# An order table of a hybrid Conformer and Mamba-2 layer: the last z tile before the LayerNorm, the last x tile after it in the list

## The chip, the core and the metric

One Trainium2 chip, one of its cores. The metric is the device time of one launch in microseconds, the median of several runs. The matrix engine is called PE (TensorE), the others DVE (VectorE), ACT (ScalarE), POOL (GpSimd); SP (SyncE) issues most DMAs.

## What is computed

One layer over a prompt of 1,040 rows (16 meta tokens and 1,024) and 32 sample rows (8 sequences of 4), model width 1,024, all in float32, followed by a gated ConvFFN and a final norm:

```python
u = _rmsnorm(h, g_mix)
proj = u @ w_in                                   # 1024 -> 4624 columns
glu = conf_in[..., :1024] * sigmoid(conf_in[..., 1024:])
c, conf_buf = _causal_dwconv(conf_prev, glu, conf_w, conf_b)      # width 31
c = silu(_layernorm(c, ln_g, ln_b))
xbc_c, xbc_buf = _causal_dwconv(xbc_prev, xbc, sconv_w, sconv_b)  # width 4
xbc_c = silu(xbc_c)                               # x (16 heads), B and C (2 groups)
y, h_ssm = _ssd(xs, dt, A, Bm, Cm, d_skip, ssm_prev)              # chunks of 128 rows
y = _group_rmsnorm(y * silu(z), snorm_g)
h = h + concat([c, y]) @ w_out
up, ffn_buf = _causal_dwconv(ffn_prev, _rmsnorm(h, g_ffn) @ w_up, fconv_w, fconv_b)
h = h + (silu(up[..., :2816]) * up[..., 2816:]) @ w_down
```

## The kernel before, in words

**Layout.** Activations lie transposed, channels on the 128 partitions and the 1,072 rows along the free axis. Every product is made of three matmuls on a split into a high and a low part (`products`, lines 215 to 217), in three column chunks of 358, 358 and 356 rows; a weight tile of 128 output columns has 8 blocks of 128 rows, so 3 x 8 x 3 = 72 matmuls make one projection tile. A weight tile is loaded (L189, `wr`), its high part made on ACT (L204, `wh`), its low part on DVE (L205, `wl`); each of these has two buffers.

**Items.** Up to the output projection the program is a list of items, `ORDER` (line 59), that a loop emits one after the other. `p0` to `p7` (`emit_pair`) are the Conformer's channel tiles: two projections, the GLU, and the convolution of width 31, made of two halves (even rows `fp`, L532 and L535; odd rows `fo`, L533 and L538) and of a third sum `fs` of both (L539, L541), put together by L544 to L547 into `gq`. `x0` to `x11` (`emit_xbc`) are the tiles of x, B and C: projection, evacuation to `fb` (L558, L560), four taps into `xo` (L575 on ACT, three L577 on DVE), silu (L579, L580), and two stores to `x_d` in memory (L581, L582). `z0` to `z7` (`emit_z`) are the gate's tiles: projection, evacuation (L589), silu (L592), store to `z_d`. `s0` and `s1` are one chunk of head group 0 or 1 of the SSD scan, which loads its x, B and C back from `x_d` (L673, L674), makes transposes (L679, L696), L697 to L700 and products; `q` is the sample rows' chunk, `r` their states. The head groups: x0 to x3, x8 and x10 are group 0's; x4 to x7, x9 and x11 are group 1's, of which x9 is its B; z4 to z7 are group 1's too. Each `l` is one block of 256 columns (the fifth has 48) of the LayerNorm over channels (`ln_part`): transposes of `gq` (L862), statistics (L863, L866), 1/sqrt (L156 on DVE, L157 on POOL, L868), normalized values `cn` (L874 on DVE, L876 on ACT), transposes back (L883), silu (L884). `h` splits the result, `c0` to `c7` are the tiles of the output projection over it.

**What sets the order.** Within an engine, instructions run in the order of its queue. A scheduler sets that order from a priority for each instruction: by default the place in the list, with some put ahead (`prio(URGENT)`: evacuations, weight splits), the taps of an x tile by a fixed 500 (`XP`), and the Conformer's taps by a fixed 1,000,000 (`CVP`), behind other work. So `ORDER` alone doesn't tell where an item comes to stand on each engine. Buffers limit it too: `fb` has two, shared with the sample chunk's `kept` and the sample state's `rr`; `xo` has two, shared with z tiles; `fp`, `fo`, `fs` and `fz` have one each.

Of the kernel before, what the change touches and what calls it, by code (L numbers as in the profile page):

```python
# [55 lines left out]
LNP = None  # L56
XP = 500
PMM, PBK, PSM = 2, 4, 2
ORDER = ("p0 p1 z1 z0 x10 p2 x8 x0 x2 p3 p4 x6 z2 p5 x3 dt x7 x1 z3 s0 s0 s0 p6 s0 s0 s0 p7 x5 x4 x11 x9 s0 q0 s0 z4 z7 z6 l l z5 l l l h s1 s1 c0 s1 r0 s1 s1 q1 s0 c2 s1 c3 s1 s1 c4 s1 s0 c5 s1 c6 y0 y1 r1 c7")


@with_exitstack
def hybrid_kernel(ctx: ExitStack, tc: tile.TileContext, a: dict, outs: list):
# [907 lines left out]
    lns, hs = ExitStack(), ExitStack()  # L971
    items = ORDER.split()
    last_ssd = max(i for i, t in enumerate(items) if t[0] in "sq")
# [571 lines left out]
```

## Time and profile before

| | |
|---|---|
| median of 3 runs | 1611.01 us (1605.16, 1611.01, 1611.17) |
| profiled execution | 1602.27 us, span 1600.6 us, mean granted PE clock 0.98 |
| PE, its weight loads | busy 96%, 92% |
| DVE, ACT, POOL | busy 73%, 56%, 3% |
| DMA | 209.90 MB, 131 GB/s over the span |

Busy shares are over the whole span, so a stage where PE waits is seen only in the windows. In the timeline, a row's first two numbers are its start and its duration in microseconds from the span's start; a bracket at the end is the idle time of the engine just before it, and what ended it.

### The profile page before, as it was taken

How to read it: one execution, taken by the hardware profiler on the slowest of the kernel's cores; microseconds unless marked ns; L12 is line 12 of the kernel's file. 1: busy time of each engine (PE TensorE's matmuls, PEld its weight loads, DVE VectorE, ACT ScalarE, POOL GpSimd, SP SyncE). 2: the span in 40 equal slices, each digit the busy share in tenths (PEclk: the TensorE clock that was granted, in tenths of full speed). 3: DMA queues.
4: the chain of work that ended last, by engine and by line, in shares of the span. 5: the costliest groups of instructions: out<-in, count | busy, mean ns of one | idle time of the engine just before them, and what ended most of it. 6: DMA issues, size and time to landing. Idle time of an engine off the chain costs nothing.

```text
span 1600.6 us, 28038 instructions
## 1 busy us (share of the span) xinstructions
PE 1536.9 (96%) x10716; PEld 1479.4 (92%) x10716; DVE 1164.3 (73%) x1881; ACT 895.7 (56%) x2160; POOL 40.4 (3%) x99
## 2 busy tenths in 40 slices
PE   6899999999999799998999999999999999999997
PEld 5899999997999688887999999999999998999997
DVE  4799989996897758465668787777777776464343
ACT  6635545478968576684335556656655665353232
POOL 2000000000000000000000000000000000000000
PEclk9999999999999899999989999999999999999998
DMA  6321312166435329667753222222222228766553
GB/s 245 112 69 58 99 45 72 57 179 160 111 115 155 101 70 268 184 172 237 241 171 107 90 84 90 81 73 70 76 83 80 83 79 273 231 204 198 154 161 108
DMA packets 306229, 209.90 MB, mean 131 GB/s; under 512 B 28453, under 2 KB 285017, under 8 KB 306079
## 3 DMA queue, kind: packets, MB, share of 16 engines
q1 hardware_dynamic: 302654, 198.26, 41.8%
q0 software_dynamic: 1056, 5.24, 0.9%
q10 hardware_dynamic: 2384, 4.60, 0.8%
q8 instruction: 84, 1.38, 0.4%
q14 instruction: 51, 0.41, 0.1%
HBM read 157.69 MB, written 51.22 MB: 131 GB/s over the span
## 4 chain that ended last, share of the span: by engine, by line
PE 81%; DMA 6%; issue 5%; DVE 4%; ACT 2%; POOL 1%; SPq 1%; POOLq 0%; DVEq 0%; ACTq 0%
PE mm L216 11%; PE mm L215 11%; PE mm L217 11%; PE X L1249 5%; PE X L1250 5%; PE X L1251 5%; PE mmd L1429 3%; PE mmd L1427 3%; PE mmd L1428 3%; PE Z L1251 2%; PE Z L1250 2%; PE Z L1249 2%; PE Y L1250 1%; PE Y L1249 1%; PE Y L1251 1%
## 5 line engine op out<-in xcount | busy, mean ns | idle before, releaser
L204 ACT CAST wh<-wr 128x768 fp32r<-128x768 f32 (+1 forms) x130 | 131.1, 1009 | 253.6 <-PE mm L216 107.1
L215 PE MATMUL mm<-u_hi,wh 128*128 128x358 f32 (+1 forms) x816 | 268.8, 329 | 0.9 <-ACT sg L245 0.9
L217 PE MATMUL mm<-u_hi,wl 128*128 128x358 f32 (+1 forms) x816 | 268.3, 329 | 0.0
L216 PE MATMUL mm<-u_lo,wh 128*128 128x358 f32 (+1 forms) x816 | 267.6, 328 | 0.0
L205 DVE TENSOR_TENSOR wl<-wr,wh 128x768 fp32r<-128x768 f32 (+1 forms) x130 | 152.4, 1173 | 109.5 <-ACT wh L204 105.2
L1250 PE MATMUL X<-tq,wh 128*128 128x264 f32 (+1 forms) x640 | 183.4, 287 | 0.0
L1249 PE MATMUL X<-tq,wh 128*128 128x264 f32 (+1 forms) x640 | 183.0, 286 | 0.0
L1251 PE MATMUL X<-tq,wl 128*128 128x264 f32 (+1 forms) x640 | 182.7, 285 | 0.0
L1429 PE MATMUL mmd<-g,wl 128*128 128x352 f32 x528 | 171.4, 325 | 1.8 <-DVE wl L205 1.8
L1427 PE MATMUL mmd<-g,wh 128*128 128x352 f32 x528 | 171.5, 325 | 0.9 <-ACT wh L204 0.9
L1428 PE MATMUL mmd<-g,wh 128*128 128x352 f32 x528 | 169.8, 322 | 0.0
L215 PEld LDWEIGHTS mm<-u_hi,wh 128*128 128x128 f32 x816 | 153.6, 188 | 1.6 <-ACT sg L245 1.1
L217 PEld LDWEIGHTS mm<-u_hi,wl 128*128 128x128 f32 x816 | 154.0, 189 | 0.6 <-issue 0.3
L216 PEld LDWEIGHTS mm<-u_lo,wh 128*128 128x128 f32 x816 | 153.5, 188 | 0.5 <-issue 0.4
L1250 PEld LDWEIGHTS X<-tq,wh 128*128 128x128 f32 x640 | 121.7, 190 | 0.0
L1249 PEld LDWEIGHTS X<-tq,wh 128*128 128x128 f32 x640 | 120.9, 189 | 0.3 <-ACT arena L1267 0.3
L1251 PEld LDWEIGHTS X<-tq,wl 128*128 128x128 f32 x640 | 121.0, 189 | 0.0
L1342 DVE SCALAR_TENSOR_TENSOR cv<-arena,ffnv,cv 128x528 f32<-128x528 f32 (+1 forms) x88 | 67.8, 771 | 65.7 <-ACT cv L1339 65.7
L1429 PEld LDWEIGHTS mmd<-g,wl 128*128 128x128 f32 x528 | 99.3, 188 | 3.4 <-DVE wl L205 3.3
L1267 ACT COPY arena<-X 128x266 f32<-128x266 f32 (+2 forms) x200 | 63.2, 337 | 69.4 <-PE X L1251 66.7
L1427 PEld LDWEIGHTS mmd<-g,wh 128*128 128x128 f32 x528 | 99.2, 188 | 1.5 <-ACT wh L204 1.1
L1428 PEld LDWEIGHTS mmd<-g,wh 128*128 128x128 f32 x528 | 99.7, 189 | 0.0
(337 smaller groups left out, 3885.8 us busy)
## 6 DMA issues: line engine op xcount, KB each, us to landing
wr<-in_w_down_dram SPq DMA_DIRECT2D x48, 512.0 KB
wr<-in_w_in_dram SPq DMA_DIRECT2D x36, 512.0 KB
wr<-in_w_out_dram SPq DMA_DIRECT2D x24, 512.0 KB
wr<-in_w_up_dram SPq DMA_DIRECT2D x24, 512.0 KB
spare<-in_w_up_dram SPq DMA_DIRECT2D x20, 512.0 KB
wr<-in_w_down_dram SPq DMA_DIRECT2D x24, 384.0 KB
ab<-acs_d SPq DMA_DIRECT2D x32, 256.0 KB
h<-in_state_ssm_dram SPq DMA_DIRECT2D x32, 256.0 KB
```

Source lines behind the costliest of these rows:

```text
L204: nc.scalar.copy(hi[:, :kk, :], raw[:, :kk, :])
L205: nc.vector.tensor_tensor(lo[:, :kk, :], raw[:, :kk, :], hi[:, :kk, :].bitcast(F), op=ALU.subtract)
L215: mm = [nc.tensor.matmul(ps[:, :n], hi[:, k, :], xh, start=(j == 0), stop=False), nc.tensor.matmul(ps[:, :n], hi[:, k, :], xl, start=False ...
L216: nc.tensor.matmul(ps[:, :n], hi[:, k, :], xl, start=False, stop=False),
L217: nc.tensor.matmul(ps[:, :n], lo[:, k, :], xh, start=False, stop=(j == kk - 1))]
L1249: tick([nc.tensor.matmul(ps[:, :n], hi[:, k, :], bh[:, k, :], start=start and k == 0, stop=False, **kw), nc.tensor.matmul(ps[:, :n], hi[:, ...
L1250: nc.tensor.matmul(ps[:, :n], hi[:, k, :], bl[:, k, :], start=False, stop=False, **kw),
L1251: nc.tensor.matmul(ps[:, :n], lo[:, k, :], bh[:, k, :], start=False, stop=(k == 3), **kw)])
L1342: nc.vector.scalar_tensor_tensor(co[:, j0:nj], fb[:, k + j0:k + nj], ffnv[:, m, 16 + k:17 + k], co[:, j0:nj], op0=ALU.mult, op1=ALU.add)
L1427: nc.tensor.matmul(ps[:, :n], hi[:, k, :], xh, start=(k0 + k == 0), stop=False)
L1428: nc.tensor.matmul(ps[:, :n], hi[:, k, :], xl, start=False, stop=False)
L1429: nc.tensor.matmul(ps[:, :n], lo[:, k, :], xh, start=False, stop=(k0 + k == KF - 1))
```

## The change

In the list, `x9` goes from behind `x11` to between the second and the third LayerNorm block, and `z5` from there to ahead of the first one. Nothing else differs.

```diff
-... s0 p7 x5 x4 x11 x9 s0 q0 s0 z4 z7 z6 l l z5 l l l h s1 s1 c0 s1 r0 ...
+... s0 p7 x5 x4 x11 s0 q0 s0 z4 z7 z6 z5 l l x9 l l l h s1 s1 c0 s1 r0 ...
```

**PE, from x11 to the first LayerNorm block.** The number behind `wh` names the weight tile: before, `wh_4782` is x9 and `wh_5666` is z5. `xc_4886` is group 0's chunk 6, `xc_5958` group 1's first chunk. Before:

```order
L217 MATMUL mm_4739<-u_hi1_126,wl_4684 128x356
L215 MATMUL mm_4786<-u_hi0_125,wh_4782 128x358
...
L679 MATMUL ptx_4889<-ident_88,xc_4886 128x128 x4
...
L215 MATMUL mm_5670<-u_hi0_125,wh_5666 128x358
...
L217 MATMUL mm_5722<-u_hi1_126,wl_5667 128x356
L696 MATMUL pbt_5978<-ident_88,xc_5958 128x128
L697 MATMUL pbt_5978<-xc_5958 128x128
L883 MATMUL pb_5565<-ident_88,cn_5541 128x128
```

With the change (`wh_5646` is x9, `wh_5151` is z4, and the one chunk 6 reads is `xc_4777`):

```order
L215 MATMUL mm_5155<-u_hi0_125,wh_5151 128x358
...
L215 MATMUL mm_5650<-u_hi0_125,wh_5646 128x358
...
L217 MATMUL mm_5702<-u_hi1_126,wl_5647 128x356
L472 MATMUL pe_5731<-ident_88,ex_4666 81x128
L862 MATMUL pt_5508<-ident_88,gq1_130 128x128
L862 MATMUL pt_5529<-ident_88,gq1_130 128x128
L696 MATMUL pbt_5978<-ident_88,xc_5958 128x128
L697 MATMUL pbt_5978<-xc_5958 128x128
L883 MATMUL pb_5543<-ident_88,cn_5519 128x128
```

x9's 72 matmuls have moved from behind x11 to the last place of the projection tiles, behind z5; they all stand ahead of the first L883, and the transposes of p7's tile (L862) stand behind them. From the first L883 on, PE's rows are the same.

**DVE, the end of p7's convolution and the first statistics.** Before:

```order
L205 TENSOR_TENSOR wl<-wr,wh 128x1024
L541 SCALAR_TENSOR_TENSOR fs<-fz,fsum,fs 128x520
L544 TENSOR_TENSOR gq_130<-fp,fo 128x520
L541 SCALAR_TENSOR_TENSOR fs<-fz,fsum,fs 128x520
L547 TENSOR_SCALAR gq_130<-cs,confv 128x32
L541 SCALAR_TENSOR_TENSOR fs<-fz,fsum,fs 128x520 x8
L545 TENSOR_TENSOR fs<-fs,fp 128x520
L546 TENSOR_TENSOR gq_130<-fs,fo 128x520
L863 BN_STATS bs<-pt 128x6 x3
```

With the change:

```order
L541 SCALAR_TENSOR_TENSOR fs<-fz,fsum,fs 128x520 x4
L205 TENSOR_TENSOR wl<-wr,wh 128x1024
L541 SCALAR_TENSOR_TENSOR fs<-fz,fsum,fs 128x520
L577 SCALAR_TENSOR_TENSOR xo<-fb,xbcv,xo 128x1096
...
L577 SCALAR_TENSOR_TENSOR xo<-fb,xbcv,xo 128x1096
L541 SCALAR_TENSOR_TENSOR fs<-fz,fsum,fs 128x520 x6
L545 TENSOR_TENSOR fs<-fs,fp 128x520
L546 TENSOR_TENSOR gq_130<-fs,fo 128x520
L816 TENSOR_TENSOR rr<-kept,rr 32x512
L863 BN_STATS bs<-pt 128x6 x3
```

x9's three taps (L577, of which one and two L541 are left out at the dots) now stand among the last L541, with six L541 and both sums behind them, and L816 of the sample states ahead of the statistics. A weight split (L205) that stood between the statistics before is ahead of the taps.

**ACT, the start of p7's convolution.** Before:

```order
L579 ACTIVATE xo<-xo 128x1040
L580 ACTIVATE fb<-xo 128x32
L532 ACTIVATE fp<-gq_130,confv 128x521
L533 ACTIVATE fo<-gq_130,confv 128x520
L744 ACTIVATE xc<-xc,dbc 128x32 x3
```

With the change:

```order
L589 COPY zo<-mm 128x358
L725 ACTIVATE ab<-ab 128x512
L724 ACTIVATE ab<-ab,acs 128x128 x4
L532 ACTIVATE fp<-gq_130,confv 128x521
L725 ACTIVATE ab<-ab 128x512
L533 ACTIVATE fo<-gq_130,confv 128x520
```

L532, on which all of p7's even taps rest, stood behind x9's silu before; now it stands behind the second evacuation of z6 (L589) and work of chunk 7.

## Rows read from the trace of the kernel before

**Rows 1.** The page: busy time (us, share of the span) and instructions of each engine, and the shares of the chain of work that ended last.

```profile
PE 1536.9 (96%) x10716; PEld 1479.4 (92%) x10716; DVE 1164.3 (73%) x1881; ACT 895.7 (56%) x2160; POOL 40.4 (3%) x99
...
PE 81%; DMA 6%; issue 5%; DVE 4%; ACT 2%; POOL 1%; SPq 1%; POOLq 0%; DVEq 0%; ACTq 0%
```

**Rows 2.** Windows of ten microseconds from x11 to the first output projection: length, busy time of PE, PEld, DVE, ACT and POOL (instructions), granted PE clock, DMA share, GB/s.

```profile
450.00:460.00 10.00, 10.00 (x63) 10.00 (x63) 9.96 (x13) 4.62 (x10) 0.10 (x1) 1.00 0.27 82
...
520.00:530.00 10.00, 10.00 (x68) 9.90 (x67) 9.76 (x16) 5.71 (x10) 0.00 (x0) 1.00 0.40 134
530.00:540.00 10.00, 5.63 (x36) 5.25 (x34) 9.31 (x20) 3.80 (x6) 1.46 (x2) 0.89 0.32 104
540.00:550.00 10.00, 6.77 (x34) 4.83 (x34) 5.42 (x14) 5.44 (x11) 1.08 (x2) 0.77 0.57 166
550.00:560.00 10.00, 8.26 (x35) 6.29 (x36) 5.21 (x9) 7.92 (x12) 0.54 (x1) 0.57 0.01 2
```

**Rows 3.** PE's timeline: x11's last matmul, x9's last and chunk 6's first, the one wait ahead of the LayerNorm, a transpose between two matmuls, and the LayerNorm.

```profile
450.64 0.33 PE L217 MATMUL mm<-u_hi,wl 128*128 128x356 f32 x1
...
462.41 0.33 PE L217 MATMUL mm<-u_hi,wl 128*128 128x356 f32 x1
462.58 0.60 PE L679 MATMUL ptx<-ident,xc 128*128 128x128 f32 x4
...
505.57 0.40 PE L780 MATMUL pn<-rs,ones 32*128 32x32 f32 x2 [0.44 <-ACT rs L779]
...
521.49 0.27 PE L862 MATMUL pt<-ident,gq 128*128 128x128 f32 x1
...
521.76 0.27 PE L862 MATMUL pt<-ident,gq 128*128 128x128 f32 x1
...
534.98 0.32 PE L217 MATMUL mm<-u_hi,wl 128*128 128x356 f32 x1
...
540.07 3.94 PE L883 MATMUL pb<-ident,cn 128*128 128x128 f32 x14 [4.44 <-DVE mv L868]
...
546.55 0.66 PE L862 MATMUL pt<-ident,gq 128*128 128x128 f32 x4 [0.66 <-ACT gq L884]
549.08 0.41 PE L883 MATMUL pb<-ident,cn 128*128 128x128 f32 x2 [1.87 <-DVE mv L156]
550.80 2.23 PE L883 MATMUL pb<-ident,cn 128*128 128x128 f32 x10 [1.31 <-ACT cn L876]
553.24 1.97 PE L862 MATMUL pt<-ident,gq 128*128 128x128 f32 x8 [0.20 <-ACT gq L884]
...
558.29 1.11 PE L862 MATMUL pt<-ident,gq 128*128 128x128 f32 x4 [0.62 <-DVE cn L874]
```

**Rows 4.** DVE's timeline at the end of p7's convolution and the start of the LayerNorm.

```profile
526.04 6.31 DVE L541 SCALAR_TENSOR_TENSOR fs<-fz,fsum,fs 128x520 f32<-128x520 f32 x8
532.39 0.70 DVE L545 TENSOR_TENSOR fs<-fs,fp 128x520 f32<-128x520 f32 x1
533.12 0.70 DVE L546 TENSOR_TENSOR gq<-fs,fo 128x520 f32<-128x520 f32 x1
533.93 1.89 DVE L863 BATCH_NORM_STATS2 bs<-pt 128x6 f32<-128x512 f32 x3
...
536.41 1.21 DVE L205 TENSOR_TENSOR wl<-wr,wh 128x1024 fp32r<-128x1024 f32 x1
537.53 0.15 DVE L156 TENSOR_SCALAR mv<-mv 128x1 f32<-128x1 f32 x1
...
538.39 0.16 DVE L868 SCALAR_TENSOR_TENSOR mv<-mv 128x1 f32<-128x1 f32 x1 [0.44 <-POOL mv L157]
```

**Rows 5.** Timeline of DVE (x11's taps among p6's, then p7's first taps), and of ACT (p7's start; then an evacuation of a z tile and two operations of chunk 7).

```profile
451.97 1.22 DVE L205 TENSOR_TENSOR wl<-wr,wh 128x1024 fp32r<-128x1024 f32 x1
...
453.80 1.36 DVE L577 SCALAR_TENSOR_TENSOR xo<-fb,xbcv,xo 128x1096 f32<-128x1096 f32 x1
455.07 0.75 DVE L541 SCALAR_TENSOR_TENSOR fs<-fz,fsum,fs 128x520 f32<-128x520 f32 x1
...
458.96 1.54 DVE L541 SCALAR_TENSOR_TENSOR fs<-fz,fsum,fs 128x520 f32<-128x520 f32 x2
...
476.01 0.74 DVE L535 SCALAR_TENSOR_TENSOR fp<-gq,confv,fp 128x521 f32<-128x521 f32 x1
...
477.29 0.74 DVE L535 SCALAR_TENSOR_TENSOR fp<-gq,confv,fp 128x521 f32<-128x521 f32 x1
477.96 0.74 DVE L538 SCALAR_TENSOR_TENSOR fo<-gq,confv,fo 128x520 f32<-128x520 f32 x1
...
472.69 0.82 ACT L532 ACTIVATE fp<-gq,confv 128x521 f32<-128x521 f32 x1 [0.62 <-DVE fs L545]
...
507.48 0.45 ACT L589 COPY zo<-mm 128x356 f32<-128x356 f32 x1
...
516.20 0.63 ACT L725 ACTIVATE ab<-ab 128x512 f32<-128x512 f32 x1
...
519.47 0.68 ACT L724 ACTIVATE ab<-ab,acs 128x128 f32<-128x128 f32 x2
```

**Rows 6.** Transfers. Timeline of SP's queue and of POOL, the last stores of x4 and of x11, and the memset of x9's buffer that waits for the first of them; then rows of the chain that ended last (start, duration, what).

```profile
448.97 0.37 SPq L582 DMA_DIRECT2D x_d<-fb  x1
...
460.75 0.37 SPq L582 DMA_DIRECT2D x_d<-fb  x1
...
451.54 0.10 POOL L552 MEMSET fb<- 128x3 f32 x1 [10.22 <-DMA x_d<-fb]
...
348.17 3.92 DMA et<-e_d
...
594.13 6.22 DMA et<-e_d
...
741.09 2.67 DMA yt<-y_d
```

**Rows 7.** A window behind the LayerNorm, columns as in rows 2.

```profile
600.00:650.00 50.00, 45.02 (x308) 40.44 (x307) 38.37 (x89) 31.45 (x106) 2.17 (x4) 1.00 0.95 265
```

**Rows 8.** Windows of four microseconds through the LayerNorm, columns as in rows 2.

```profile
536.00:540.00 4.00, 0.00 (x0) 0.00 (x0) 3.56 (x11) 2.52 (x5) 1.46 (x2) 0.72 0.38 123
540.00:544.00 4.00, 3.80 (x15) 2.54 (x16) 1.32 (x2) 3.19 (x7) 0.00 (x0) 0.50 1.03 273
544.00:548.00 4.00, 2.56 (x19) 2.08 (x17) 2.91 (x7) 1.44 (x3) 0.54 (x1) 0.92 0.41 141
```

More of the change, by code (lines that the diff above doesn't have):

```diff
@@ L58 @@
 PMM, PBK, PSM = 2, 4, 2
-ORDER = ("p0 p1 z1 z0 x10 p2 x8 x0 x2 p3 p4 x6 z2 p5 x3 dt x7 x1 z3 s0 s0 s0 p6 s0 s0 s0 p7 x5 x4 x11 x9 s0 q0 s0 z4 z7 z6 l l z5 l l l h s1 s1 c0 s1 r0 s1 s1 q1 s0 c2 s1 c3 s1 s1 c4 s1 s0 c5 s1 c6 y0 y1 r1 c7")
+ORDER = ("p0 p1 z1 z0 x10 p2 x8 x0 x2 p3 p4 x6 z2 p5 x3 dt x7 x1 z3 s0 s0 s0 p6 s0 s0 s0 p7 x5 x4 x11 s0 q0 s0 z4 z7 z6 z5 l l x9 l l l h s1 s1 c0 s1 r0 s1 s1 q1 s0 c2 s1 c3 s1 s1 c4 s1 s0 c5 s1 c6 y0 y1 r1 c7")
 @with_exitstack
```

## The prediction

> **What bounds the kernel now.** I read the page's busy times and its chain first: TensorE (PE) is busy for 1536.9 of 1600.6 us, and 81% of the chain that ended last is PE [rows 1]. Time can be won only in PE's gaps, some 64 us in all, and lost only by making new ones. The windows show where the change lies beside a gap: PE is full up to 530 us, busy for 5.63, 6.77 and 8.26 us of the next three stretches of ten, and its granted clock falls to 0.57 there [rows 2]. PE's timeline names that gap. x11's gemm ends at 450.97 and x9's runs to 462.74; chunk 6 follows (L679), and up to the last projection matmul of z5, which ends at 535.30, PE waited once, for 0.44 us [rows 3]. Then come the LayerNorm's back transposes (L883) with its statistics in between, and there PE waits 4.44 + 0.66 + 1.87 + 1.31 + 0.20 + 0.62 = 9.1 us [rows 3].
>
> What the LayerNorm waits for stands on VectorE (DVE). p7's convolution ends with eight taps (L541) and two sums (L545, L546), the last at 533.12 + 0.70 = 533.82; the first statistics (L863) start at 533.93 and the first L883 at 540.07 [rows 3, 4], 6.25 us behind L546. So the convolution and the last projection tile end within 1.5 us of each other, and the one that moves back moves the LayerNorm.
>
> **What the order says the change is.** By the order, x9's gemm does not get inside the LayerNorm. Its 72 matmuls leave their place behind x11 and become the last projection tile, behind z5, and all still stand ahead of the first L883; from there on PE's order is the old one. What goes between the first LayerNorm blocks in the list gets onto PE ahead of them, because their statistics wait for p7 anyway. On DVE x9's three taps (L577) now stand in front of the last six L541, L545 and L546 of p7, where before they stood 60 us earlier. DVE runs its queue in order, so the LayerNorm's inputs now wait for x9's gemm.
>
> **The sum, part by part.**
>
> *PE ahead of the LayerNorm.* 72 matmuls leave at 451 and come back at the end. A gemm takes 462.74 - 450.97 = 11.77 us in either place, at full clock in both [rows 2, 3]: 0. Since PE was unbroken but for 0.44 us, the end of the projections stays at E = 535.3. Chunk 6, the sample chunk and their loads start 11.8 us earlier; if one of them is late, PE waits and E moves back, above by as much as the longest such wait nearby, 3.92 us for a load in the chain at 348 us [rows 6]; below, the 0.44 goes and E is 0.4 earlier. I take 0, since no load held PE anywhere from 451 to 535 us [rows 3].
>
> *DVE behind E.* x9's end is followed by the same steps as x11's was: weight split (L205), an L541, the first L577. There the first L577 started at 453.80, 2.83 us behind the gemm's end at 450.97, and the three L577 with two L541 between them and up to the next L541 took 458.96 - 453.80 = 5.16 us [rows 3, 5]. Then the six L541, 6/8 of 6.35 us (526.04 to 532.39) = 4.76, and L545 and L546, 533.82 - 532.39 = 1.43 [rows 4]. L546 ends at 535.30 + 2.83 + 5.16 + 4.76 + 1.43 = 549.5 instead of 533.8: **+15.7 us**.
>
> *DVE itself late.* ScalarE's start of p7's taps (L532, 472.69 before [rows 5]) now stands behind z6's second evacuation. That is 168 matmuls at 0.163 us and 14 transposes before E, each of which adds 0.11 to its matmul (0.27 from start to start [rows 3]), so near 506.4; with the evacuation, L725, four L724 and its own 0.82 us (0.35, 0.54, 1.4 of ScalarE's queue [rows 5]) the first tap is at about 509.6, instead of 476.0 [rows 5]. From there DVE has 29 taps of the two halves at 0.67 (477.29 to 477.96), six L541 (4.5 us), two sums (0.75) and two L205 at 1.14 [rows 4, 5]: 27.0 us, so 536.6 against the 536.3 at which L205 can start. **+0.3**, between 0 (the cover holds) and 2 (a stall of DVE in chunk 7). That cover is gone: these taps had 24 us more before.
>
> *The LayerNorm's own chain.* A weight split of 1.1 us leaves it (L205 at 536.41 to 537.53 [rows 4]), and the sample state's L816 comes in ahead of L863, a DVE operation of 0.6 us: **-0.5**. L816 also needs x9's store, below.
>
> *Clock.* PE's idle stretch ahead of L883 grows from 4.44 us to about 20. The clock was 0.72 in the four microseconds of idling and 0.50 (1.2 of 2.4 GHz) in those behind, where PE did the first transposes, and it came back to 0.92 behind them [rows 8]. So the first transposes are at the low level in both kernels. Below: 0. Above: both the transposes and the first matmuls behind them run longer at half speed, at most the 3.94 us of that first row again [rows 3]. I take **+0.5**, near the lower end, since the clock is low already in the row before.
>
> *Behind the LayerNorm.* Order and work are unchanged and PE is the bound there, so the delay is carried: 0. What could give it back is a rival.
>
> *Items with one answer.* z5's gemm, evacuations and store are 11.8 us earlier, and nothing in the LayerNorm reads them: 0. The first w_out loads keep their place relative to the last projection tile: 0.
>
> Sum 15.7 + 0.3 - 0.5 + 0.5 = **16.0 us**, from the profiled 1602.3 to 1618.3. The profiled execution is 8.7 us below the median of the three runs (1611.0); on the median that is 1611.0 + 16.0 = **1627**.
>
> There is a rule that speaks for the change. In the trace, PE's waits lie in the LayerNorm, and DVE is busy there for 5.42 and 5.21 us of ten, while just ahead of it PE is full and DVE nearly so, 9.76 us [rows 2]. The Trainium skill, Perfetto Trace Analysis, section Optimization Strategy, says that where the most-contended engine changes over time, interleaving such regimes may improve performance; by it the sum would be a gain of up to the 9.1 us that PE waits. The order doesn't interleave here: it puts the tile's DVE work ahead of the regime it should fill, so I go by the rows.
>
> **The rivals.**
>
> *It does what it says (faster).* If x9's gemm filled PE's waits in the LayerNorm and its taps ran behind the convolution, PE would win at most 9.1 us [rows 3], and DVE would lose three taps of 1.27 us ahead of L546 [rows 5]: 1611.0 - 9.1 = 1602. It decides if at least one of x9's three column chunks (24 matmuls, 3.9 us) ran behind the first L883. For it: the words of the change. Against it: PE's and DVE's queues are in order, and no row of x9 stands behind L883. Chance 0.06.
>
> *Given back later (no change).* DMA's busy share is 0.95 from 600 to 650 us and PE waits for 4.98 us there [rows 7], with a 6.22 us wait for a transfer in the chain ahead of it [rows 6]. If these transfers don't shift with the LayerNorm, up to 5 us come back there, which alone leaves 11; if later waits for transfers (the chain has some up to 6 us) give back 3 to 11 more, 0 to 8 us are left: 1611 to 1619. It decides from 8 us given back. Against it: the loads wait for buffers of chunks that shift as well. Chance 0.13.
>
> *x9's way through memory gates the LayerNorm (slower still).* Head group 1's first chunk reads x9's output back (L674), and its L696 stands ahead of L883 on PE, its copy L698 ahead of the LayerNorm's on ScalarE, its L700 ahead of L868 on DVE. x11's last store was issued at 460.75, 9.78 us behind its gemm's end, so x9's would be at 545.1; a store landed 451.54 - 448.97 = 2.57 us behind its issue, and a load read back from memory took 2.67 to 6.22 in the chain [rows 6], so the data is there at 550.3 to 553.9. It is needed some 4.6 us behind L546 (L868 at 538.39 before [rows 4]), at 554.1. The margin is 0.2 to 3.8 us: not binding, but a late store makes it so, at up to +28: 1639. L816 needs the store alone, at 547.6 against 549.5. Chance 0.12.
>
> **How the numbers follow.** The forecast has 0.69, with its own range from the bounds of the terms (E -0.4 to +3.9, DVE late -0.3 to +1.7, clock -0.5 to +3.4 against what I took, which won't all meet): +14.5 to +23, 1625 to 1634, and down to 1621 because the three runs of before differ by 6 us among themselves. The 8-in-10 range leaves out the faster rival and the half of the second one that is nearest to no change (0.12 together) and the far end of the third (some 0.05): 1613 to 1638. About 0.5% (8 us) is what a measurement of this kernel tells from no change: slower 0.69 + 0.12 = 0.81, same 0.13, faster 0.06.
>
> **What would show it.** Right: L546 of p7 ends near 549.5; PE stands idle for about 20 us between x9's last L217, near 535, and the first L883 near 556; DVE waits or is just in time at L205 and L577; behind the LayerNorm the stretches are as long as before. The term for DVE is wrong if L205 starts behind 538. The faster rival shows as L217 of x9 between two L883, the second rival as a PE idle time from 600 to 680 that shrinks, the third as L696, L700 or L816 waiting for x_d or xc. The prediction is wrong if L546 ends before 540.

## The result

| | before | changed |
|---|---|---|
| median | 1608.94 us (4 runs, 1605.16 to 1611.17) | 1625.86 us (4 runs, 1625.39 to 1628.95) |
| profiled execution's span | 1600.6 us | 1623.7 us |
| mean granted PE clock | 0.98 | 0.972 |

The ratio of the runs is 1.0116, with an interval from 1.0095 to 1.0138 (the medians alone give 1.0105): slower by about 1%, 16.9 us of medians. The forecast was 16.0 us more, 1627, in a range from 1613 to 1638.

The page of the changed kernel: busy time of each engine.

```profile
PE 1545.1 (95%) x10716; PEld 1485.2 (91%) x10716; DVE 1164.9 (72%) x1881; ACT 896.2 (55%) x2160; POOL 40.4 (2%) x99
```

DVE and ACT are as busy as in [rows 1], PE by 8 us more for the same 10716 matmuls, which goes with its lower mean clock (0.972 against 0.98). The other 15 us of the 23.1 between the two profiles are PE's idling. The windows show where, columns as in [rows 2]:

```profile
520.00:530.00 10.00, 10.00 (x68) 9.91 (x67) 10.00 (x15) 2.97 (x4) 0.00 (x0) 1.00 0.45 129
530.00:540.00 10.00, 5.87 (x35) 5.38 (x34) 9.89 (x15) 3.53 (x8) 0.00 (x0) 0.94 0.27 86
540.00:550.00 10.00, 0.21 (x1) 0.21 (x2) 9.72 (x13) 3.02 (x6) 0.00 (x0) 0.50 0.48 146
550.00:560.00 10.00, 4.20 (x17) 2.81 (x17) 7.05 (x18) 3.40 (x7) 1.46 (x2) 0.50 0.12 45
560.00:570.00 10.00, 6.41 (x32) 5.26 (x30) 4.94 (x12) 4.96 (x9) 1.08 (x2) 0.67 0.01 2
570.00:580.00 10.00, 7.71 (x43) 6.37 (x42) 6.78 (x10) 6.17 (x10) 0.54 (x1) 0.85 0.00 0
```

Between 540 and 550 us PE stands and DVE is full. PE's timeline names what it waits for (`...` marks rows left out):

```profile
535.21 0.33 PE L217 MATMUL mm<-u_hi,wl 128*128 128x356 f32 x1
537.17 0.34 PE L472 MATMUL pe<-ident,ex 128*81 128x128 f32 x1 [1.64 <-ACT ex L567]
549.79 0.69 PE L862 MATMUL pt<-ident,gq 128*128 128x128 f32 x2 [12.28 <-DVE gq L546]
...
555.58 0.66 PE L883 MATMUL pb<-ident,cn 128*128 128x128 f32 x2 [4.47 <-DVE mv L156]
557.56 3.26 PE L883 MATMUL pb<-ident,cn 128*128 128x128 f32 x12 [1.32 <-ACT cn L876]
...
564.02 0.66 PE L862 MATMUL pt<-ident,gq 128*128 128x128 f32 x4 [0.66 <-ACT gq L884]
```

x9's gemm ends at 535.54 (z5's ended at 535.30 [rows 3]); the first transpose that needs p7's convolution waits 12.28 us for L546, and the first L883 starts at 555.58 instead of 540.07. DVE and ACT ahead of that:

```profile
508.69 0.81 ACT L532 ACTIVATE fp<-gq,confv 128x521 f32<-128x521 f32 x1
...
535.40 1.05 ACT L204 CAST wh<-wr 128x1024 fp32r<-128x1024 f32 x1 [3.28 <-PE mm L216]
...
537.03 1.30 ACT L575 ACTIVATE xo<-fb,xbcv 128x1096 f32<-128x1096 f32 x1
```

```profile
509.54 1.56 DVE L535 SCALAR_TENSOR_TENSOR fp<-gq,confv,fp 128x521 f32<-128x521 f32 x2 [5.56 <-ACT fp L532]
...
536.58 1.22 DVE L205 TENSOR_TENSOR wl<-wr,wh 128x1024 fp32r<-128x1024 f32 x1
...
538.38 1.35 DVE L577 SCALAR_TENSOR_TENSOR xo<-fb,xbcv,xo 128x1096 f32<-128x1096 f32 x1
...
542.27 1.35 DVE L577 SCALAR_TENSOR_TENSOR xo<-fb,xbcv,xo 128x1096 f32<-128x1096 f32 x1
...
548.30 0.70 DVE L545 TENSOR_TENSOR fs<-fs,fp 128x520 f32<-128x520 f32 x1
549.04 0.70 DVE L546 TENSOR_TENSOR gq<-fs,fo 128x520 f32<-128x520 f32 x1
549.77 0.68 DVE L816 TENSOR_TENSOR rr<-kept,rr 32x512 fp32r<-32x512 f32 x1
550.48 1.89 DVE L863 BATCH_NORM_STATS2 bs<-pt 128x6 f32<-128x512 f32 x3
...
554.64 0.80 DVE L874 TENSOR_SCALAR cn<-pt,mv 128x512 f32<-128x512 f32 x1
555.36 0.14 DVE L156 TENSOR_SCALAR mv<-mv 128x1 f32<-128x1 f32 x1
...
556.53 0.16 DVE L868 SCALAR_TENSOR_TENSOR mv<-mv 128x1 f32<-128x1 f32 x1 [0.44 <-POOL mv L157]
```

p7's convolution starts at 508.69 on ACT where before it started at 472.69 [rows 5], and its first tap waits 5.56 us for that start. From there to the first statistics (L863) no row of DVE has a wait in brackets, not the L205, not the taps of x9 and none of those left out: DVE was late by itself, and x9's gemm was ready for it. It was ready only just: L205 needs ACT's L204, which waits for x9's gemm and ends at 536.45, and L205 starts at 536.58; the first L577 needs L575, which ends at 538.33, and starts at 538.38. Two ways of being late end here within 0.2 us of each other, and that is what the experiments had to take apart.

### The profile page after: what moved, and what is told of

It is laid out like the page before. It is cut to its first block, busy times and chain, and to the rows that moved or that the text cites. A ratio compares the mean times of both kernels' runs of the same rounds, so it can differ in the third digit from the quotient of the medians.

```text
span 1623.7 us, 28036 instructions
## 1 busy us (share of the span) xinstructions
PE 1545.1 (95%) x10716; PEld 1485.2 (91%) x10716; DVE 1164.9 (72%) x1881; ACT 896.2 (55%) x2160; POOL 40.4 (2%) x99
## 4 chain that ended last, share of the span: by engine, by line
PE 52%; issue 7%; DMA 4%; DVE 2%; ACT 2%; POOL 1%; SPq 0%; POOLq 0%; DVEq 0%; ACTq 0%
PE X L1249 5%; PE X L1250 5%; PE X L1251 5%; PE mmd L1429 3%; PE mmd L1427 3%; PE mm L215 3%; PE mmd L1428 3%; PE mm L216 3%; PE mm L217 3%; PE Z L1251 2%; PE Z L1250 2%; PE Z L1249 2%; PE Y L1250 1%; PE Y L1249 1%; PE Y L1251 1%
## 5 line engine op out<-in xcount | busy, mean ns | idle before, releaser
L204 ACT CAST wh<-wr 128x768 fp32r<-128x768 f32 (+1 forms) x130 | 131.0, 1009 | 250.7 <-PE mm L216 104.5
L205 DVE TENSOR_TENSOR wl<-wr,wh 128x768 fp32r<-128x768 f32 (+1 forms) x130 | 152.5, 1173 | 110.6 <-ACT wh L204 109.8
```

Of the source, the lines that this page charges most:

```text
L204: nc.scalar.copy(hi[:, :kk, :], raw[:, :kk, :])
L205: nc.vector.tensor_tensor(lo[:, :kk, :], raw[:, :kk, :], hi[:, :kk, :].bitcast(F), op=ALU.subtract)
```

## The experiments

Two theories give the same time for the changed kernel. **A** is the prediction's: x9's gemm is the last projection tile, and its taps stand in front of p7's last sums. **B**: ACT starts p7's convolution 36 us late, and DVE, full from there, can't finish it in time. Every ratio below is to runs of the kernel before on the same chip.

**One part alone: only z5 moved.**

```diff
-... x11 x9 s0 q0 s0 z4 z7 z6 l l z5 l l l h ...
+... x11 x9 s0 q0 s0 z4 z7 z6 z5 l l l l l h ...
```

> Only z5 is moved ahead of the LayerNorm blocks in the list; x9 stays behind x11. Theory A (the prediction: x9's gemm, last of the projection tiles, and its three taps in front of p7's last sums hold the LayerNorm) expects no change, within 3 us of before, since z5 is the last projection tile on PE in both. Theory B (ScalarE starts p7's convolution 33 us late because x9's gemm no longer stands behind x11, and DVE is full from there) expects the same: the start of p7's convolution keeps its place. A third theory, that moving z5 costs something of its own, expects a part of the 17 us, 5 or more.

1609.2 us, ratio 1.0001 (0.9985 to 1.0017). z5's part of the change costs nothing by itself; the loss comes with x9's.

**x9's taps taken out of the way.** A dependency on DVE alone puts the three L577 of x9 behind L546 (the edit shortened, here and below where angle brackets or a comment stand for code).

```diff
-            nc.vector.tensor_tensor(ca[:, :, 1], pz, po_, op=ALU.subtract)
+            last["L546"] = nc.vector.tensor_tensor(ca[:, :, 1], pz, po_, op=ALU.subtract).ins
...
+                    # each of x9's three taps, instruction t
+                    tc.add_manual_dep(t, last["L546"].name, <no semaphore, order only>)
```

> The changed kernel with x9's three DVE taps held behind p7's last sum (L546); x9's gemm is still the last projection tile and p7's convolution still starts late. Theory A expects the LayerNorm to start with the end of PE's projections again: L546 ends near 537 to 540, and the time is 1609 to 1613 us. Theory B expects only the three taps to go: 3 x 1.27 = 3.8 us, L546 at 545.9 instead of 549.7, and 1622 us, still 13 above before.

1624.51 us, ratio 1.0105 (1.0082 to 1.0127): the loss stays. DVE and PE of this kernel (ahead of it, this execution had lost some 8.6 us to the lower clock, so times are to be read against each other):

```profile
554.62 0.70 DVE L546 TENSOR_TENSOR gq<-fs,fo 128x520 f32<-128x520 f32 x1
555.24 1.35 DVE L577 SCALAR_TENSOR_TENSOR xo<-fb,xbcv,xo 128x1096 f32<-128x1096 f32 x1
```

```profile
544.22 0.33 PE L217 MATMUL mm<-u_hi,wl 128*128 128x356 f32 x1
...
555.38 0.69 PE L862 MATMUL pt<-ident,gq 128*128 128x128 f32 x2 [8.86 <-DVE gq L546]
563.01 0.66 PE L883 MATMUL pb<-ident,cn 128*128 128x128 f32 x2 [6.94 <-DVE mv L156]
```

L546 ends at 555.32, 10.8 us behind the end of the gemm (544.55), where the changed kernel has 549.74 - 535.54 = 14.2. So 3.4 us come back, about the 3.8 of three taps, and no more. About 2 of them are lost again: the taps now stand among the statistics, and the first L883 starts 7.7 us behind L546 instead of 5.8. Of the 15.7 us by which the change moved L546 against the end of the gemm (before, it was 1.5 ahead of it), 12.3 are left. Only the taps are out of the way here: an L205 that needs the end of x9's gemm still stands ahead of the last nine L541, at 545.59, but it doesn't wait.

**x9's gemm taken off the end.**

```diff
-... x11 s0 q0 s0 z4 z7 z6 z5 l l x9 l l l h ...
+... x11 s0 q0 s0 z4 z7 z6 x9 z5 l l l l l h ...
```

> The changed kernel with x9 ahead of z5 in the list, both ahead of the LayerNorm: x9's gemm ends 11.8 us earlier, so its taps need not wait for the end of the projections, and p7's convolution still starts late on ScalarE. Theory A expects the wait for x9 to be gone and the LayerNorm to start at the end of z5's gemm: 1609 to 1614 us. Theory B expects DVE to have the same work behind the same late start: L546 near 549 to 551, 1624 to 1627 us, no better than the changed kernel.

1631.45 us, ratio 1.0125 (1.009 to 1.0161). x9's taps ran from 528.94 on, long before the gemm of z5 ended (537.74), and L546 was later still. p7's first tap had started at 513.11, again behind a wait of 5.57 us for L532, and operations of group 1's first chunk (L700, L726) now stood ahead of the sums:

```profile
537.41 0.33 PE L217 MATMUL mm<-u_hi,wl 128*128 128x356 f32 x1
...
556.68 0.69 PE L862 MATMUL pt<-ident,gq 128*128 128x128 f32 x2 [15.86 <-DVE gq L546]
```

Theory A falls as the sole cause: without x9 at the end the loss is as large.

**The late start undone.** The changed kernel, with L532 and L533 of p7 at the priority of an evacuation.

```diff
-            nc.scalar.activation(pe_, ..., scale=wv(0), bias=wv(31))
-            nc.scalar.activation(po_, ..., scale=wv(1))
+            with prio(URGENT if i == 7 else tc.cur_priority): nc.scalar.activation(pe_, ..., scale=wv(0), bias=wv(31))
+            with prio(URGENT if i == 7 else tc.cur_priority): nc.scalar.activation(po_, ..., scale=wv(1))
```

> The changed kernel with one thing undone: ScalarE's two starts of p7's convolution (L532, L533) get the priority of an evacuation, so that they stand some 29 us earlier in its queue. In the order the convolution is then through before x9's taps, and x9's matmuls stand between the first L883. Theory B expects the whole loss back, L546 at 530 to 534 and 1609 us or less; if x9's gemm then fills PE's waits in the LayerNorm, up to 9 us less than before, 1600 to 1609. Theory A in its strict form (x9's late end is what counts, through its read-back by head group 1 and its gemm, not the convolution's start) expects 1618 to 1626.

1612.01 us, ratio 1.0016 (0.9999 to 1.0033): the loss is gone, to some 3 us that can't be told from none. L532 starts at 481.61, and x9's matmuls now do run inside the LayerNorm. But nothing is won against before. PE's waits in this kernel (total us, times, longest us):

```profile
PE pb L883 <- DVE cn L874: 6.1, 3, 2.9
PE pt L862 <- ACT gq L884: 2.2, 3, 1.4
```

and DVE's rows there:

```profile
545.79 1.36 DVE L577 SCALAR_TENSOR_TENSOR xo<-fb,xbcv,xo 128x1096 f32<-128x1096 f32 x1 [0.22 <-ACT xo L575]
547.07 0.15 DVE L868 SCALAR_TENSOR_TENSOR mv<-mv 128x1 f32<-128x1 f32 x1
547.14 0.69 DVE L863 BATCH_NORM_STATS2 bs<-pt 128x6 f32<-128x512 f32 x1
547.75 1.34 DVE L577 SCALAR_TENSOR_TENSOR xo<-fb,xbcv,xo 128x1096 f32<-128x1096 f32 x1
549.01 0.81 DVE L874 TENSOR_SCALAR cn<-pt,mv 128x512 f32<-128x512 f32 x1
549.73 1.35 DVE L577 SCALAR_TENSOR_TENSOR xo<-fb,xbcv,xo 128x1096 f32<-128x1096 f32 x1
```

x9's taps have moved in between the second block's statistics and its normalization, which PE waits for.

**The late start alone, on the kernel before.** Its list stays, x9 behind x11; p7's convolution is emitted as an item of its own, and its three starts depend on z7's last evacuation on ACT (order only) at the priority of an evacuation.

```diff
-... x11 x9 s0 q0 s0 z4 z7 z6 l l z5 ...
+... x11 x9 s0 q0 s0 z4 z7 k7 z6 l l z5 ...
+                # L532, L533, L539 of p7, instruction t
+                tc.add_manual_dep(t, last["z", 7, 2].name, <no semaphore, order only>)
```

> The kernel before, its list unchanged and x9 behind x11; only ScalarE's starts of p7's convolution (L532, L533, L539) are held until z7's last evacuation, near 508 us, where the change put them. Theory B (the late start alone makes the loss) expects DVE to be full from about 509: 45 taps at 0.67 to 0.79, three weight splits, chunk 7's operations and the sums, so L546 near 547 to 551 and 1621 to 1627 us. Theory A (x9's gemm as the last tile, with its taps in front) expects no loss without x9 there: 1608 to 1612 us.

1624.25 us, ratio 1.0096 (1.0069 to 1.0124): a loss of the same size, without moving x9. L532 starts at 513.66, L546 ends at 553.40, and PE is idle for 14.56 us:

```profile
538.24 0.33 PE L217 MATMUL mm<-u_hi,wl 128*128 128x356 f32 x1
...
553.46 0.69 PE L862 MATMUL pt<-ident,gq 128*128 128x128 f32 x2 [14.56 <-DVE gq L546]
```

Theory B is sufficient. The start is not quite that of the change: it comes 24.9 us ahead of the end of the projections (538.57), where the changed kernel has 26.9, and x9's taps are not there; the two make up for each other. That B is also necessary e4 doesn't show by itself, since with the early start x9's taps left their place in front of the sums as well.

**What took the gain back in e4.** e4 with x9's three DVE taps left out of the computation.

> The kernel of the early start (e4) with x9's three DVE taps left out of the computation, so that nothing of x9 stands on DVE in the LayerNorm. In e4 x9's matmuls stood in the LayerNorm and nothing was won against before. If the taps among the LayerNorm's statistics gave the gain back (PE waited 6.1 us there for DVE's L874), expect 4 to 6 us less than e4: 1604 to 1608. If x9's gemm was too nearly through when the LayerNorm began, and the LayerNorm waits for its own chain, expect 1610 to 1613 as in e4.

1607.0 us, ratio 0.998 (0.9961 to 0.9999), some 5 us below e4's 1612.0: the taps among the statistics cost what the filling won.

**The convolution ahead of all.** The changed kernel with all of p7's convolution at the x tiles' tap priority.

```diff
-        with prio(CVP if CVP is not None else tc.cur_priority):
+        with prio(XP if i == 7 else CVP):
```

> The changed kernel with the whole of p7's convolution (starts, taps and sums) at the priority of an x tile's taps, so that DVE runs it in one piece from about 480 us and chunk 7 and the sample chunk get DVE behind it. Expect L546 at 524 to 528, first L883 some 20 matmuls ahead of x9's end, and, if that fills PE's waits, 1600 to 1606 us; if x9's taps or the chunks' delayed DVE work take it back, 1607 to 1614.

1607.47 us, ratio 1.0006 (0.9987 to 1.0026). L546 ends at 523.44, 15.7 us ahead of the projections' end (539.15), and the first L883 runs at 532.23 among x9's matmuls. PE's waits again have L874 at the top, which x9's taps hold up as in e4:

```profile
PE pb L883 <- DVE cn L874: 6.4, 4, 2.9
```

**Both: the convolution ahead, x9's taps behind a LayerNorm block.** In e8 and e9 x9's taps, silu and stores are an item of their own, with a DVE dependency on the last L874 emitted before it.

```diff
-... z5 l l x9 l l l h ...
+... z5 l l x9 k9 l l l h ...      e8: behind the second block
+... z5 l l x9 l k9 l l h ...      e9: behind the third block
```

> The kernel of e7 (p7's convolution in one piece) with x9's taps and what follows them (silu, stores) held behind the second LayerNorm block's normalization on DVE, so that they no longer stand among the statistics of the second block. In e7 PE waited 6.4 us for L874 there. If the taps among the statistics were what took the gain back, expect 3 to 6 us less than e7: 1601 to 1605 us, below before. If the wait only moves (head group 1's first chunk or the third block waits instead), 1606 to 1611.

> As e8, with x9's taps held one block later, behind the third block's normalization: by then PE has output projections to do beside the LayerNorm. Same expectation, 1601 to 1605 us if the taps among the statistics took the gain back; 1606 to 1612 if head group 1's first chunk, which reads x9's output, comes too late for it.

e8: 1604.62 us, ratio 0.997 (0.9951 to 0.999). e9: 1604.03 us, ratio 0.9975 (0.9953 to 0.9998). Both beat both kernels, by 4 to 5 us against before, with intervals that end just below 1. PE's wait for the normalization on DVE is smaller (in these two files L874 is L878 and L883 is L887), here in e8:

```profile
PE pb L887 <- DVE cn L878: 3.9, 5, 2.1
```

The kernel before with its own list and the convolution ahead was not run, so how much of the 4 to 5 us needs x9 in its new place is not shown.

**The changed kernel again.**

> The changed kernel once more, unaltered, for a second profile. The first profile was 23.1 us longer than that of before, the medians 16.9. If the 6 us between them are a low granted clock of varying length in the sample rows' chunks (before: 0.66 for ten microseconds of head group 1's; the changed kernel: 0.78, 0.71 and 0.83 for thirty) and not the change's, expect the way from p7's L546 to the end of the LayerNorm to repeat within 1 us, and the clock there, and with it the span, to differ by some microseconds; the median again 1624 to 1628. If they are the change's, expect the same clock dip and the same span within 1 us.

1625.96 us, ratio 1.0083 (1.0051 to 1.0114), span of the profile 1635.0. The LayerNorm repeats to the hundredth (first L577 to L546: 543.68 to 554.34, 10.66 us in both; PE's wait for L546 12.28 and 12.3), and what differs lies elsewhere: this execution was 5 us behind the first profile before x9's taps, and lost 3.4 us more to the clock from 640 to 660 (0.89 and 0.77, where the first had 1.00 at the same place). The clock dip in head group 1's sample chunk is there in both, 0.77, 0.71 and 0.83 against 0.78, 0.71 and 0.83. So the expectation held for the LayerNorm and not for the dip, whose length in the changed kernel was the same twice.

## Why the prediction was right, and where it was not

The forecast was 1.1 us above the measured median (1627 against 1625.86) and the difference 0.9 us below the measured one, and nearly every term was right:

- E, the end of the projections: 535.3 forecast, 535.54 found. Moving 72 matmuls cost PE nothing, as said.
- DVE: first tap at 509.6 forecast and 509.54 found, L205 at 536.6 and 536.58, L546's end at 549.5 and 549.74.
- The LayerNorm's own chain: -0.5 forecast. Ahead of the first L883 it is 5.84 us instead of 6.25, -0.4. But the term stops there, and the first block has a second half: its L156 stood ahead of L726 and L874 before (538.46) and stands behind them now (555.36, first DVE lines above), so its L868 comes at 556.53, and PE waits 1.32 us for its values (L876), where before it had no wait between the two halves. With that the term is +0.9.
- The clock: +0.5 forecast. The first L883 is 15.5 us late, and the last block 17.4 by the offset of the same matmuls in both traces. Of these 1.9 us, 1.3 are the wait just named. The other 0.6 goes with the clock, 0.50 and 0.67 from 550 to 570, where PE does the first transposes: close to the value taken.
- Together: L546 ends 15.9 us later, and -0.4 + 1.3 + 0.6 make 17.4 at the end of the LayerNorm.
- Behind the LayerNorm nothing was given back: the same matmuls are 17.4 us late at 651 us of before as well; the rival that it would be (0.13) is out. x9's way through memory did not bind: the longest wait there is for L546 and for the statistics.

DVE in the kernel before, at the second half of the first block:

```profile
538.46 0.15 DVE L156 TENSOR_SCALAR mv<-mv 128x1 f32<-128x1 f32 x1
538.52 0.68 DVE L726 TENSOR_TENSOR ab<-ab,cbm 128x512 f32<-128x512 f32 x1
539.12 0.80 DVE L874 TENSOR_SCALAR cn<-pt,mv 128x512 f32<-128x512 f32 x1
539.85 0.15 DVE L868 SCALAR_TENSOR_TENSOR mv<-mv 128x1 f32<-128x1 f32 x1
```

**The step that failed is the attribution.** The prediction put 15.7 us on x9's gemm and its taps and +0.3 on DVE's own lateness, as a cover that was just gone. The trace has no wait of DVE for x9. A late start of p7's convolution alone makes a loss of that size on the kernel before (e5: 15.5 us), and with it x9 can go ahead (e3) or its taps behind (e2) without getting more than 3.4 us of the way to the LayerNorm back. The sum was right because both ways ended at the same place, 536.3 against 536.6 at L205: that it came out is luck as far as the cause goes. The prediction's sign for being right, that DVE waits or is just in time at L205 and L577, holds for both ways and couldn't tell them apart. The working had both numbers and called the second one a correction to the first; with two ways that close, each has to be followed to the end without the other. That x9's late gemm with a punctual convolution would cost as much is not shown: as soon as the start was early, the order put x9's taps behind the sums (e4), so that case wasn't tried.

The faster rival was a real possibility that this change missed: e8 and e9 win 4 to 5 us when the LayerNorm's input is early and the filling tile's DVE work stays out of its chain. The rule of the Trainium skill (Perfetto Trace Analysis, section Optimization Strategy), that interleaving stages whose most-contended engine differs may improve performance, agrees with these two runs, with 4 to 5 of the 9.1 us, as far as the gain is the filling's.

The 23.1 us between the two profiles, against 16.9 of the medians, come from behind the LayerNorm. The same matmuls are 17.4 us late at 651 us of before and 22.1 at 702, over head group 1's sample chunk. Before and after, columns as in [rows 2]:

```profile
660.00:670.00 10.00, 9.98 (x96) 9.24 (x96) 1.49 (x5) 5.90 (x18) 0.54 (x1) 1.00 0.67 187
670.00:680.00 10.00, 10.00 (x52) 9.60 (x51) 3.90 (x12) 4.99 (x19) 0.33 (x1) 0.66 0.54 149
680.00:690.00 10.00, 9.64 (x70) 7.57 (x70) 5.27 (x17) 8.13 (x33) 0.75 (x2) 1.00 0.61 148
```

```profile
680.00:690.00 10.00, 9.98 (x79) 9.29 (x77) 1.16 (x3) 5.45 (x18) 0.00 (x0) 0.78 0.49 133
690.00:700.00 10.00, 10.00 (x50) 9.29 (x50) 4.30 (x13) 4.94 (x19) 0.54 (x1) 0.71 0.42 134
700.00:710.00 10.00, 9.64 (x61) 8.09 (x61) 4.43 (x14) 6.90 (x29) 0.54 (x1) 0.83 0.65 151
```

The lost clock is 0.34 of ten microseconds before, and 0.22 + 0.29 + 0.17 = 0.68 of ten after, so 3.4 against 6.8 us. Whether the change lengthens that dip is open: both profiles of the changed kernel have it long, and only one of the kernel before was taken. Of the other profiles, e1 has 3.4 us there and e4, e5 and e7 have 6.8; since e7 is as fast as before, the long dip is not the mark of the loss.

## What to carry to other kernels

Taking a tile's gemm out of its place can delay, by the scheduler's order, work that has no link to it. Here that work had low priority, and a higher one alone brought it back from 508.69 to 481.61 (e4). So when an item of a list is moved, look for what ran in its shadow, here the two activations by which ACT starts the last convolution. And to fill a gap of PE, the work that the gap waits for has to be early, and the tile that fills it must not bring its own vector work into the chain that made the gap.

## What the runs showed of the hardware

PE's granted clock falls without PE being idle. In the kernel before, PE was busy for 9.98 and 10.00 of ten microseconds from 660 to 680. The small matmuls and transposes of head group 1's sample chunk (32 L800 from 653.8, 64 L803 to 670.7), with gemm matmuls among them, ran at 1.00 up to 670; from 672 to 676 the clock was 0.50, and a gemm matmul behind them took 0.50 us instead of 0.33. In the changed kernel it fell at about 686, before the last L803 (690.2), and was 0.50 up to 694. In e2 it happened in head group 0's sample chunk as well, where the kernel before and the changed one had 1.00, and cost that execution some 8.6 us, as in e8 (8.5) and e9 (3.4). In e2:

```profile
470.00:480.00 10.00, 10.00 (x58) 9.70 (x58) 5.13 (x9) 2.31 (x5) 0.54 (x1) 0.65 0.46 132
480.00:490.00 10.00, 10.00 (x41) 9.95 (x42) 2.39 (x5) 5.65 (x13) 0.00 (x0) 0.50 0.19 57
```

So one execution can lie several microseconds from the median of its kernel (the profiled one of e8 took 1616.48 us, the median of its twelve runs is 1604.62), and a difference of 0.3% needs many runs.
